# Residual rows of a hybrid decoder layer: turned by VectorE in the up product in place of TensorE after the cross attention, and another order of the last output pair

## The chip, the cores and the metric

The kernel runs on one core of a Trainium2 chip. The metric is device time in microseconds of one execution, as the median of several runs. Before the change it is 1285.01 us (three runs, 1284.41 to 1285.12). One further execution was profiled; the trace that is quoted below comes from it.

## The reference, cut to what matters

One decoder layer over 1024 tokens of width 1024, all in float32: a token mixer (linear attention beside sliding-window attention), a cross attention to 256 memory tokens, a gated MLP with a causal convolution of width 3, and a last RMSNorm. What bears on the change is the end of it:

```python
h = h + concat([o_gla, o_swa]) @ w_out
h = h + cross_attn(rms_norm(h, norm_cross), rms_norm(mem, norm_mem), w_q_c, w_k_c, w_v_c, w_o_c)
h = h + conv_ffn(rms_norm(h, norm_ffn), w_up, conv_w, conv_b, w_down)   # u = h @ w_up; conv; silu(gate) * val; @ w_down
return rms_norm(h, norm_final)
```

The `h` after the second line, called h2 in the kernel, is used twice: normalised, as the input of the up product, and as it is, as the residual that is added to the down product.

## The kernel before, in words

**Layout.** Activations are kept transposed: eight tiles of 128 features x 1024 tokens (`self.h2[0..7]`). The down product comes out with tokens on the partitions, so its residual is wanted in rows: token tile x features. The kernel turns h2 into that form and stores it in a DRAM tensor `h2_d` (eight tiles of 128 tokens x 1024 features), from which the down product's `snapshot` loads 128x512 pieces late in the program.

**Products.** Every matrix product is made of three passes of `fp32r` matmuls on a high and a low part (high x high, high x low, low x high), 128x512 each. Most weights go through a block scheme with seven products of half size in place of eight (Strassen-Winograd): `out_pair` computes two feature tiles of h2 with seven products named "1" to "7", each of 12 matmuls, in the order of a string; `up_winograd` does the same for a gate tile and a value tile of the MLP.

**Cross attention's output.** `cross_out` runs `out_pair` for the pairs j = 1, 2, 3 (tiles 2j and 2j+1; pair 0 was done before). Each pair uses three PSUM banks of a role ("F" or "S", three banks each), and the products that add to an earlier one share its bank. After each product a generator `between` gives other work a step. In the kernel before these steps are calls of `out_rows`: four TensorE transposes 128x128 into the bank of role "T" (L1604), a ScalarE copy to SBUF (L1607) and a POOL DMA to `h2_d` (L1608). There are 16 such calls (8 tiles, 2 halves): twelve lie in the three pairs and four in the eight steps behind them.

Behind the pairs stands the first half (tokens 0 to 511) of the first gate and value tiles of the MLP, not by blocks: eight steps k, each of 2 banks x 3 matmuls (L149 to L151), on h2 that is scaled with the gain but not yet with the row factor. Between the steps stand the remaining transposes, `rstd_half` (the row factors of 512 tokens: 8 small matmuls, L213, then a chain of small VectorE and ScalarE operations, L183 to L191) and `broadcast_rows` (8 small matmuls, L205, and a ScalarE copy to the tile `bc`, L207). Then `ffn_norm` scales the h2 tiles in place with `bc` (VectorE, L1700) and splits them into high and low parts (ScalarE L110 and L113, VectorE L111 and L114); the half with tokens 512 to 1023 is used first, by `up_plain`.

**The up product.** For j = 2 to 21 a block: PE runs the seven products of a gate and a value tile (84 matmuls, L1790). ScalarE and VectorE empty the banks (L1833 to L1845), run the convolution (L1852, L1854), the SiLU and the gate (L1863, L1864), and POOL stores the result to `g_d` (L1865). In the same block they prepare weights: SP loads two tiles of 512 KB (`g`, L1753, and `v`, L1754) into a pool `st` of three buffers, ScalarE and VectorE split them and their sums into high and low parts (L110, L111; sums L1771 to L1776). A load waits until its buffer's last reader is done. PSUM banks alternate between the roles "F" and "S" from block to block.

**What sets the order.** In the stages around `out_pair` the order on TensorE is that in which the code calls; a scheduler of the framework orders the other engines, and all engines in the up product. Each engine then runs its list in that order and waits at semaphores. SP and POOL hold their DMA issues in one list each. The pool `pre` has six buffers of 128x1024; in the kernel before they hold the first operands of the down product.

Of the kernel before, what the change touches and what calls it, by code (L numbers as in the profile page):

```python
# [28 lines left out]
P = 128  # L29
# [32 lines left out]
class Layer:  # L62
# [1484 lines left out]
        product(1, 1, 1)  # L1547
        yield

    def out_pair(self, j, weights, h, tmp, role, order, between):  # L1550


        nc = self.nc
# [1 line left out]
        b11, b21, b22, w1, w2, w3, w4 = weights  # L1555
        left = dict(zip("1234567", (b11, b21, b22, w4, w1, w2, w3)))
        right = dict(zip("1234567", (self.wo[n] for n in ("a11", "a12", "s4", "a22", "s1", "s2", "s3"))))
        banks = [self.bank(role) for _ in range(3)]
        at = dict(zip(order, (0, 1, 0, 2, 0, 2, 0) if j == 1 else (0, 1, 2, 0, 1, 2, 0)))
        t0, t1 = slice(0, 512), slice(512, 1024)  # L1560
        v1, u2, s5 = (tmp("c", [P, 512], bufs=3) for _ in range(3))

# [33 lines left out]
                out(0, t1, ps, v1, ALU.subtract)  # L1596
            next(between, None)

    def out_rows(self, tile, half, tmp):

        nc = self.nc
        ps = self.bank("T")
        for i in range(4):
            nc.tensor.transpose(ps[:, i * P:(i + 1) * P], self.h2[tile][:, (4 * half + i) * P:(4 * half + i + 1) * P],  # L1604
                                self.ident)
        t = tmp("h2r", [P, 4, P], bufs=2)
        nc.scalar.copy(out=t, in_=ps)  # L1607
        nc.gpsimd.dma_start(out=self.h2_d[4 * half:4 * half + 4, :, tile * P:(tile + 1) * P].rearrange("i p c -> p i c"),  # L1608
                            in_=t)

    def cross_out(self, new, tmp, o8, weights, bc):


        nc = self.nc
        self.h2_d = self.dram.tile([NT, P, T], F32, name="h2_d")
        rf = self.small("rstd", [P, NT])
        u = []
        last = NK // 2 - 1

        def rows(j):  # L1620
            for tile in (2 * j, 2 * j + 1):
                for half in range(2):
                    self.out_rows(tile, half, tmp)
                    yield

        def turn(j, which):

            hi, lo = (new("q", [P, 2, 512], F32R, 8) for _ in range(2)) if which[0] == 0 else u.pop()
            for i in which:
                self.split(self.h2[2 * j + i][:, 0:512], hi[:, i], lo[:, i], self.v("norm_ffn", 2 * j + i))  # L1630
            u.append((hi, lo))

        def first_rows():
            g = rows(0)
            for step in (0, 1, 1, 0, 1, 1):
                if step:
                    next(g)
                yield

        def last_rows():  # L1640
            g = rows(last - 1)
            next(g)
            yield
            next(g)
            turn(0, (0, 1))
            yield
            next(g)
            turn(1, (0, 1))
            yield
            next(g)  # L1650
            turn(2, (0, 1))
            yield
            yield
            turn(last, (0,))
            yield
            yield

        for j in range(1, last + 1):
            self.out_tiles(o8)
            self.out_pair(j, weights, self.h2[2 * j:], tmp, "FS"[j % 2], "1426573" if j == 1 else "1652734",  # L1660
                          first_rows() if j == 1 else rows(j - 1) if j < last else last_rows())
            if j < last:
                *_, weights = self.out_weights(j + 1, new)
            if j == last - 1:
                weights = [weights, self.plain_weights(0)]
                weights, plain = weights
        turn(last, (1,))
        banks = [self.bank("F") for _ in range(2)]
        g = rows(last)
        between = {0: lambda: self.rstd_half(rf, self.ss, 0), 1: lambda: next(g), 2: lambda: self.rstd_half(rf, self.ss, 1),  # L1670
                   3: lambda: self.broadcast_rows(rf, bc, (0,), role="S"),
                   4: lambda: self.broadcast_rows(rf, bc, (1,), role="S"), 5: lambda: next(g), 6: lambda: next(g),
                   7: lambda: next(g)}
        for k in range(NK):
            hi, lo = u[k // 2]
            for (wh, wl), ps in zip(plain, banks):
                self.mm3(ps, wh[:, k], wl[:, k], hi[:, k % 2], lo[:, k % 2], k == 0, k == NK - 1)
            between[k]()
        return plain, banks


# [176 lines left out]
    def ffn_up(self, j, us, new):  # L1858

        nc = self.nc  # L1860
        yg = self.conv(us[0], j, new)
        yv = self.conv(us[1], NJ + j, new)
        last = nc.scalar.activation(out=yg, in_=yg, func=AF.Silu)  # L1863
        nc.vector.tensor_tensor(out=yg, in0=yg, in1=yv, op=ALU.mult)  # L1864
        nc.gpsimd.dma_start(out=self.g_d[j], in_=yg)  # L1865
        return last

# [297 lines left out]
    def run(self):  # L2165
# [40 lines left out]
        with self.banks(F=3, S=3, T=1, O=1):  # L2206
# [13 lines left out]
            with self.pool("a", "right") as anew, self.pool("u", "right") as new, ExitStack() as wxs:  # L2220
# [26 lines left out]
                with self.pool("xy") as xnew:  # L2247
                    for j in range(NPLAIN, NJ):
                        if j > NPLAIN:
                            *_, weights = ahead if j == NPLAIN + 1 else self.up_weights(j, wnew)  # L2250
                            us = self.up_winograd(j, weights, new, xnew)
                        if j == NJ - 1:
                            down = self.ffn_down(pre, hcnew)
                            next(down)
# [31 lines left out]
```

## Time and profile before

| what | value |
|---|---|
| median of the runs | 1285.01 us (1284.41 to 1285.12) |
| the profiled execution | 1285.49 us |
| its span in the trace | 1283.8 us |
| PE busy | 1269.5 us, 99% of the span |
| VectorE (DVE) busy | 989.2 us, 77% |
| ScalarE (ACT) busy | 632.8 us, 49% |
| GpSimd (POOL) busy | 114.2 us, 9% |
| DMA | 159.79 MB, 124 GB/s in the mean |
| the three output pairs | 572.6 to 635.6 us from the span's start |
| the eight steps behind them | 635.6 to 651.9 us |
| the up product by blocks | about 685 to 1060 us, 19.04 us each |

The profiled execution is 1.7 us longer than its span; the trace has no row for what lies around the span. PE is the queue of matmuls, PEld the loading of their weights. A row of the timeline has the start, the length, engine and line, tiles (out<-in), and in square brackets how long the engine sat idle before and what it waited for. Matmuls are pipelined: a single one has a length of 0.39 us, though the next starts 0.227 us later, so distances of starts say more than lengths.

### The profile page before, as it was taken

Reading aid. Unit: us, or ns where it says so; the run is one execution under the profiler, and the core shown is the slowest. Engines: PE = TensorE matmul, PEld = TensorE weight load, DVE = VectorE, ACT = ScalarE, POOL = GpSimd, SP = SyncE. Lnnn points to the kernel's source line nnn. Section 1 sums busy time; section 2 is a strip of 40 time slices with the busy share of each in tenths; the row PEclk is TensorE's granted clock in tenths of the full one; section 3 lists DMA queues with packets and bytes.
Section 4 is the critical chain, followed back from the end, with each engine's and each line's share of the span. In section 5 each row is a group of like instructions: output and inputs, shape, how many; then the busy total and the mean of one; then the engine's idle time right before and its main releaser. Section 6 shows DMA issues by size and latency. Waiting matters only on the chain.

```text
span 1283.8 us, 17649 instructions
## 1 busy us (share of the span) xinstructions
PE 1269.5 (99%) x6619; PEld 1059.5 (83%) x6619; DVE 989.2 (77%) x1704; ACT 632.8 (49%) x1127; POOL 114.2 (9%) x194
## 2 busy tenths in 40 slices
PE   8999999999999999999999999999999999999997
PEld 8887777888888888888888888888888888888886
DVE  6848764358657876896898988888888876999687
ACT  5525445336534534864556544344344444454455
POOL 1400111101122000001131000000000000000001
PEclk9999999999999999999999999999999999999999
DMA  7641211238754354243365434222322339610204
GB/s 227 186 122 56 73 58 58 70 132 295 223 156 132 119 167 169 105 141 119 118 146 118 151 102 131 86 72 90 96 68 82 99 113 340 236 66 9 74 19 155
DMA packets 138605, 159.79 MB, mean 124 GB/s; under 512 B 16289, under 2 KB 100438, under 8 KB 138518
## 3 DMA queue, kind: packets, MB, share of 16 engines
q1 hardware_dynamic: 122678, 111.02, 27.6%
q0 software_dynamic: 15680, 47.36, 11.4%
q8 instruction: 52, 0.85, 0.3%
q14 instruction: 35, 0.29, 0.1%
q10 hardware_dynamic: 160, 0.27, 0.1%
HBM read 113.26 MB, written 42.48 MB: 121 GB/s over the span
## 4 chain that ended last, share of the span: by engine, by line
PE 97%; DVE 1%; ACT 1%; DMA 0%; issue 0%; SPq 0%; DVEq 0%; ACTq 0%
PE psS L1790 15%; PE psF L1790 14%; PE psF L149 8%; PE psF L150 7%; PE psF L151 7%; PE psF L1940 6%; PE psS L1940 6%; PE psF L1291 5%; PE psS L1568 3%; PE psS L149 3%; PE psS L151 3%; PE psS L150 3%; PE psO L1940 2%; PE psT L1940 2%; PE psF L1568 1%; PE psO L149 1%
## 5 line engine op out<-in xcount | busy, mean ns | idle before, releaser
L110 ACT CAST w<-st 128x1024 fp32r<-128x1024 f32 (+1 forms) x147 | 125.9, 858 | 212.9 <-PE psF L150 41.1
L111 DVE TENSOR_TENSOR w<-st,w 128x1024 fp32r<-128x1024 f32 (+1 forms) x147 | 144.0, 981 | 55.5 <-ACT w L110 55.4
L1854 DVE SCALAR_TENSOR_TENSOR uy<-uy,vec,uy 128x1023 f32<-128x1023 f32 (+1 forms) x88 | 111.9, 1278 | 0.7 <-ACT uy L1852 0.4
L1790 PE MATMUL psS<-a,w 128*128 128x512 f32 x384 | 92.4, 389 | 0.0
L1940 PE MATMUL psF<-w,w 128*128 128x512 f32 x318 | 88.9, 389 | 0.0
L1940 PE MATMUL psS<-w,w 128*128 128x512 f32 x312 | 87.4, 389 | 0.0
L1790 PEld LDWEIGHTS psS<-a,w 128*128 128x128 f32 x384 | 72.1, 188 | 14.9
L149 PE MATMUL psF<-xh,w 128*128 128x512 f32 x208 | 83.0, 399 | 0.0
L151 PE MATMUL psF<-xh,w 128*128 128x512 f32 x208 | 81.5, 392 | 0.0
L150 PE MATMUL psF<-xl,w 128*128 128x512 f32 x208 | 81.2, 390 | 0.0
L1790 PE MATMUL psF<-a,w 128*128 128x512 f32 x336 | 80.7, 389 | 0.0
L1790 PEld LDWEIGHTS psF<-a,w 128*128 128x128 f32 x336 | 63.1, 188 | 13.1
L1940 PEld LDWEIGHTS psF<-w,w 128*128 128x128 f32 x318 | 59.7, 188 | 12.4
L1940 PEld LDWEIGHTS psS<-w,w 128*128 128x128 f32 x312 | 58.6, 188 | 12.1
L1852 ACT ACTIVATE uy<-uy,vec 128x1024 f32<-128x1024 f32 x44 | 54.8, 1246 | 21.1 <-DVE uy L1845 17.8
L1790 PE MATMUL psS<-act,wx 128*128 128x512 f32 x252 | 60.5, 389 | 0.0
L1790 PE MATMUL psS<-act,w 128*128 128x512 f32 x240 | 58.0, 389 | 0.0
L1790 PE MATMUL psF<-act,w 128*128 128x512 f32 x240 | 57.8, 390 | 0.0
L1790 PEld LDWEIGHTS psS<-act,wx 128*128 128x128 f32 x252 | 47.3, 188 | 9.8
L1790 PE MATMUL psF<-act,wx 128*128 128x512 f32 x228 | 54.8, 389 | 0.0
L1790 PEld LDWEIGHTS psF<-act,w 128*128 128x128 f32 x240 | 45.0, 188 | 9.8 <-ACT o L1815 0.5
L1790 PEld LDWEIGHTS psS<-act,w 128*128 128x128 f32 x240 | 45.1, 188 | 9.3
(574 smaller groups left out, 3071.6 us busy)
## 6 DMA issues: line engine op xcount, KB each, us to landing
st<-in_w_up_dram SPq DMA_DIRECT2D x44, 512.0 KB, 3.7
g_d<-uy POOLq DMA_DIRECT2D x22, 512.0 KB, 2.9
act<-in_w_down_dram SPq DMA_DIRECT2D x12, 512.0 KB, 9.7
st<-g_d SPq DMA_DIRECT2D x10, 512.0 KB, 3.8
res<-g_d SPq DMA_DIRECT2D x10, 512.0 KB, 9.2
st<-in_w_in_dram SPq DMA_DIRECT2D x9, 512.0 KB, 6.8
xt_d<-pts POOLq DMA_DIRECT2D x16, 256.0 KB, 5.4
ow_d<-pts POOLq DMA_DIRECT2D x32, 128.0 KB, 2.8
```

Source lines behind the costliest of these rows:

```text
L110: h = nc.scalar.copy(out=hi, in_=src)
L111: l = nc.vector.tensor_tensor(out=lo, in0=src, in1=hi.bitcast(F32), op=ALU.subtract)
L149: mm(out, lhsT=lh, rhs=rh, start=start, stop=False, skip_group_check=joined)
L150: mm(out, lhsT=lh, rhs=rl, start=False, stop=False, skip_group_check=joined)
L151: mm(out, lhsT=ll, rhs=rh, start=False, stop=stop, skip_group_check=joined)
L1291: mm(ps[n], lhsT=left[n][l][:, q], rhs=self.qa[right[n]][q][r], start=new and q == 0 and i == 0, stop=new and q == 3 and i == 2, skip_grou ...
L1568: mm(ps, lhsT=left[n][l][:, q], rhs=right[n][q][r], start=new and q == 0 and i == 0, stop=new and q == 3 and i == 2, skip_group_check=not new)
L1790: self.nc.tensor.matmul(ps, lhsT=b[l][:, q], rhs=a[q][r], start=first and q == 0 and n == 0, stop=first and q == 3 and n == 2, skip_group_ ...
L1852: nc.scalar.activation(out=y, in_=u, func=AF.Identity, scale=self.v("cw2", j), bias=self.v("conv_b", j))
L1854: nc.vector.scalar_tensor_tensor(out=y[:, s:], in0=u[:, :T - s], scalar=self.v(nm, j), in1=y[:, s:], op0=ALU.mult, op1=ALU.add)
L1940: nc.tensor.matmul(ps[i], lhsT=g[:, l, tk], rhs=w[:, r], start=first and k == 0 and m == 0, stop=first and k == n - 1 and m == 2, skip_gro ...
```

## The change

The TensorE transposes, their ScalarE copies and the stores of `out_rows` are gone. In their place:

- `cross_out` stores the eight h2 tiles as they are (features x tokens, 512 KB each) to a new DRAM tensor `h2t_d`, by POOL, behind the last pair.
- In the up product's blocks j = 6 to 13, behind the gate's multiplication of that block, `row_form` takes one tile k = j - 6: SP loads it from `h2t_d` into a `pre` buffer, VectorE transposes the 32x32 squares inside it into a second `pre` buffer (two instructions 128x512), and POOL issues eight DMAs that put the squares at their places in `h2_d`. Each of those DMAs moves 32 partitions x 16 runs of 32 floats, that is 512 runs of 128 bytes, 64 KB. A buffer of `pre` is now used by `row_form` first and by the down product's loads after it.
- The last output pair (j = 3) runs in the order "1657243" in place of "1652734", with product 4 in a bank of role "T". The outputs for tokens 512 to 1023 are then complete one product earlier.
- In the eight steps behind it the row factors of the second half (tokens 512 to 1023) come behind k = 2 and their broadcast behind k = 4; those of the first half behind k = 5 and k = 7.

```diff
-    def out_pair(self, j, weights, h, tmp, role, order, between):
+    def out_pair(self, j, weights, h, tmp, role, order, homes, between):
...
-        banks = [self.bank(role) for _ in range(3)]
-        at = dict(zip(order, (0, 1, 0, 2, 0, 2, 0) if j == 1 else (0, 1, 2, 0, 1, 2, 0)))
+        banks = [self.bank(r) for r in (role, role, role, "T")[:max(homes) + 1]]
+        at = dict(zip(order, homes))
...
-    def out_rows(self, tile, half, tmp):
-        nc = self.nc
-        ps = self.bank("T")
-        for i in range(4):
-            nc.tensor.transpose(ps[:, i * P:(i + 1) * P], self.h2[tile][:, (4 * half + i) * P:(4 * half + i + 1) * P],
-                                self.ident)
-        t = tmp("h2r", [P, 4, P], bufs=2)
-        nc.scalar.copy(out=t, in_=ps)
-        nc.gpsimd.dma_start(out=self.h2_d[4 * half:4 * half + 4, :, tile * P:(tile + 1) * P].rearrange("i p c -> p i c"),
-                            in_=t)
+    def row_form(self, k, pre):
+        nc = self.nc
+        src, dst = (pre("pre", [P, T], F32, 6) for _ in range(2))
+        nc.sync.dma_start(out=src, in_=self.h2t_d[k])
+        rows = self.h2_d.rearrange("i (b r) c -> r (i b) c", r=32)
+        for h in range(2):
+            sl = slice(512 * h, 512 * h + 512)
+            nc.vector.transpose(out=dst[:, sl], in_=src[:, sl])
+            for a in range(4):
+                c = k * P + 32 * a
+                nc.gpsimd.dma_start(out=rows[:, 16 * h:16 * h + 16, c:c + 32],
+                                    in_=dst[32 * a:32 * a + 32, sl].rearrange("r (b s) -> r b s", s=32))
...
-            self.out_pair(j, weights, self.h2[2 * j:], tmp, "FS"[j % 2], "1426573" if j == 1 else "1652734",
-                          first_rows() if j == 1 else rows(j - 1) if j < last else last_rows())
+            self.out_pair(j, weights, self.h2[2 * j:], tmp, "FS"[j % 2],
+                          *(("1426573", (0, 1, 0, 2, 0, 2, 0)) if j == 1 else ("1652734", (0, 1, 2, 0, 1, 2, 0))
+                            if j < last else ("1657243", (0, 1, 2, 1, 0, 3, 2))), turns() if j == last else iter(()))
...
+        for k in range(NK):
+            nc.gpsimd.dma_start(out=self.h2t_d[k], in_=self.h2[k])
...
-        between = {0: lambda: self.rstd_half(rf, self.ss, 0), 1: lambda: next(g), 2: lambda: self.rstd_half(rf, self.ss, 1),
-                   3: lambda: self.broadcast_rows(rf, bc, (0,), role="S"),
-                   4: lambda: self.broadcast_rows(rf, bc, (1,), role="S"), 5: lambda: next(g), 6: lambda: next(g),
-                   7: lambda: next(g)}
+        between = {2: lambda: self.rstd_half(rf, self.ss, 1), 4: lambda: self.broadcast_rows(rf, bc, (1,), role="S"),
+                   5: lambda: self.rstd_half(rf, self.ss, 0), 7: lambda: self.broadcast_rows(rf, bc, (0,), role="S")}
...
+                        if 6 <= j < 6 + NK:
+                            with self.tc.issue_after(self.gated.ins):
+                                self.row_form(j - 6, pre)
```

The scheduler moves rows with it. Line numbers of the changed program are smaller from here on (L1700 is L1683, L1835 is L1818, L1864 is L1847, L1754's sums L1771 to L1776 are L1754 to L1759). The first place is VectorE where the row factors of the two halves are made, behind the last pair. Before (`rs_v`, `rs_t` and `rstd` are the row factors, `o` the h2 tiles, `bc` the broadcast factors, `act` the low parts):

```order
L189 TENSOR_TENSOR rs_t_6418<-rs_t_6418,rs_v_6417 128x4
L190 TENSOR_SCALAR rs_t_6418<-rs_t_6418 128x4
L191 TENSOR_TENSOR rstd_5874<-rs_y_6419,rs_t_6418 128x4
L188 TENSOR_TENSOR rs_t_6453<-rs_y_6454 128x4
L189 TENSOR_TENSOR rs_t_6453<-rs_t_6453,rs_v_6452 128x4
L190 TENSOR_SCALAR rs_t_6453<-rs_t_6453 128x4
L191 TENSOR_TENSOR rstd_5874<-rs_y_6454,rs_t_6453 128x4
L1700 SCALAR_TENSOR_TENSOR o_5736<-o_5736,vec,bc_5870 128x512
```

After:

```order
L1683 SCALAR_TENSOR_TENSOR o_5738<-o_5738,vec,bc_5870 128x512
L183 TENSOR_SCALAR rs_v_6382<-psO_6377 128x4
L111 TENSOR_TENSOR act_6436<-o_5736,act_6435 128x512
L111 TENSOR_TENSOR act_6436<-o_5738,act_6435 128x512
L188 TENSOR_TENSOR rs_t_6383<-rs_y_6384 128x4
L1683 SCALAR_TENSOR_TENSOR o_5876<-o_5876,vec,bc_5870 128x512
L189 TENSOR_TENSOR rs_t_6383<-rs_t_6383,rs_v_6382 128x4
L1683 SCALAR_TENSOR_TENSOR o_5878<-o_5878,vec,bc_5870 128x512
L190 TENSOR_SCALAR rs_t_6383<-rs_t_6383 128x4
L111 TENSOR_TENSOR act_6438<-o_5876,act_6437 128x512
L191 TENSOR_TENSOR rstd_5875<-rs_y_6384,rs_t_6383 128x4
```

Before, the row factors of both halves stand together, ahead of all scaling. After, those of the first half (`rs_v_6382` to the second `rstd_5875`) stand between scalings and splits of the second half's tiles.

The second place is VectorE in one block of the up product (`c` and `uy` are the emptying of the banks and the convolution, `st` the loaded weights, `w` and `wx` their low parts). Before:

```order
L1835 TENSOR_TENSOR c_7965<-psF_7968,c_7964 128x512
L1864 TENSOR_TENSOR uy_7927<-uy_7927,uy_7931 128x1024
L1771 TENSOR_TENSOR st_8073<-st_8073 128x512
L1775 TENSOR_TENSOR st_8073<-st_8073,st_8072 128x512
L1776 TENSOR_TENSOR st_8072<-st_8072,st_8073 128x512
L111 TENSOR_TENSOR w_8093<-st_8072,w_8092 128x1024
L1839 TENSOR_TENSOR c_7966<-psF_7968,c_7964 128x512
L111 TENSOR_TENSOR wx_8089<-st_8073,wx_8088 128x1024
L1841 TENSOR_TENSOR uy_7963<-psF_7969,c_7966 128x512
```

After:

```order
L1818 TENSOR_TENSOR c_7752<-psS_7755,c_7751 128x512
L1847 TENSOR_TENSOR uy_7714<-uy_7714,uy_7718 128x1024
L1607 STREAM_TRANSPOSE pre_7849<-pre_7848 128x512 x2
L1754 TENSOR_TENSOR st_7873<-st_7873 128x512
L1758 TENSOR_TENSOR st_7873<-st_7873,st_7872 128x512
L1759 TENSOR_TENSOR st_7872<-st_7872,st_7873 128x512
L1822 TENSOR_TENSOR c_7753<-psS_7755,c_7751 128x512
L111 TENSOR_TENSOR wx_7889<-st_7873,wx_7888 128x1024
L111 TENSOR_TENSOR w_7893<-st_7872,w_7892 128x1024
L1824 TENSOR_TENSOR uy_7750<-psS_7756,c_7753 128x512
```

The two transpositions stand right behind the gate's multiplication, and the split of `w`, whose end frees a buffer for the next load, comes two instructions later, behind the emptying L1822 and the split of `wx`.

The third place is SP's queue over three of these blocks. Before:

```order
L1754 DMA st_7269<-in_w_up_dram 128x8x128
L1753 DMA st_7402<-in_w_up_dram 128x8x128
L1886 DMA pre_9542<-g_d 128x2x512
L1754 DMA st_7403<-in_w_up_dram 128x8x128
L1753 DMA st_7536<-in_w_up_dram 128x8x128
```

After:

```order
L1736 DMA st_7578<-in_w_up_dram 128x8x128
L1603 DMA pre_7554<-h2t_d 128x1024
L1737 DMA st_7579<-in_w_up_dram 128x8x128
L1736 DMA st_7725<-in_w_up_dram 128x8x128
L1603 DMA pre_7701<-h2t_d 128x1024
L1737 DMA st_7726<-in_w_up_dram 128x8x128
```

The load of a tile of h2 stands between the loads of the gate's and of the value's weights, and the down product's first loads, which shared these places before, stand behind all eight tiles.

More of the change, by code (lines that the diff above doesn't have):

```diff
@@ L1615, in cross_out @@
         self.h2_d = self.dram.tile([NT, P, T], F32, name="h2_d")
+        self.h2t_d = self.dram.tile([NK, P, T], F32, name="h2t_d")
         rf = self.small("rstd", [P, NT])
@@ L1618, in cross_out @@
         last = NK // 2 - 1
[L1620 to L1624, printed above, removed]
         def turn(j, which):
@@ L1631, in turn, with turns @@
             u.append((hi, lo))
[L1633 to L1637, printed above, removed]
-                yield
[L1640 to L1652, printed above, removed]
+        def turns():
+            yield
+            for j in range(3):
+                turn(j, (0, 1))
+                yield
             yield
@@ L1667, in cross_out @@
         turn(last, (1,))
+        for k in range(NK):
+            nc.gpsimd.dma_start(out=self.h2t_d[k], in_=self.h2[k])
         banks = [self.bank("F") for _ in range(2)]
-        g = rows(last)
-        between = {0: lambda: self.rstd_half(rf, self.ss, 0), 1: lambda: next(g), 2: lambda: self.rstd_half(rf, self.ss, 1),
-                   3: lambda: self.broadcast_rows(rf, bc, (0,), role="S"),
-                   4: lambda: self.broadcast_rows(rf, bc, (1,), role="S"), 5: lambda: next(g), 6: lambda: next(g),
-                   7: lambda: next(g)}
+        between = {2: lambda: self.rstd_half(rf, self.ss, 1), 4: lambda: self.broadcast_rows(rf, bc, (1,), role="S"),
+                   5: lambda: self.rstd_half(rf, self.ss, 0), 7: lambda: self.broadcast_rows(rf, bc, (0,), role="S")}
         for k in range(NK):
@@ L1677, in cross_out @@
                 self.mm3(ps, wh[:, k], wl[:, k], hi[:, k % 2], lo[:, k % 2], k == 0, k == NK - 1)
-            between[k]()
+            if k in between:
+                between[k]()
         return plain, banks
@@ L1863, in ffn_up @@
         last = nc.scalar.activation(out=yg, in_=yg, func=AF.Silu)
-        nc.vector.tensor_tensor(out=yg, in0=yg, in1=yv, op=ALU.mult)
+        self.gated = nc.vector.tensor_tensor(out=yg, in0=yg, in1=yv, op=ALU.mult)
         nc.gpsimd.dma_start(out=self.g_d[j], in_=yg)
```

## The prediction

> **What bounds the kernel now.** I read the page first: busy time by engine, then the chain that ended last.
>
> ```profile
> PE 1269.5 (99%) x6619; PEld 1059.5 (83%) x6619; DVE 989.2 (77%) x1704; ACT 632.8 (49%) x1127; POOL 114.2 (9%) x194
> ...
> PE 97%; DVE 1%; ACT 1%; DMA 0%; issue 0%; SPq 0%; DVEq 0%; ACTq 0%
> ```
>
> PE sets the time: it is busy for 99% of the span and makes 97% of the chain. Work taken off PE is worth its full length; work added elsewhere costs only where it makes PE wait. So I ask two things: what leaves PE, and which of the added or moved steps can come too late for it. The places are then read from the timelines: PE's in the output pairs and the eight steps, VectorE's and SP's in one block of the up product.
>
> **The change part by part. 1: transpositions leave PE.** PE's timeline at the start of the three pairs, at the eight steps and behind them, and last the group of the removed matmuls (lines by form, 570 to 680 us):
>
> ```profile
> 572.62 4.24 PE L1568 MATMUL psS<-act,w 128*128 128x512 f32 x18
> 576.71 1.53 PE L1568 MATMUL psS<-q,w 128*128 128x512 f32 x6
> 578.07 0.60 PE L1604 MATMUL psT<-ident,o 128*128 128x128 f32 x4
> 578.42 3.01 PE L1568 MATMUL psS<-act,w 128*128 128x512 f32 x12
> 581.27 0.60 PE L1604 MATMUL psT<-ident,o 128*128 128x128 f32 x4
> ...
> 635.59 0.39 PE L149 MATMUL psF<-q,w 128*128 128x512 f32 x1
> ...
> 636.95 0.95 PE L213 MATMUL psO<-ones,ss 128*128 128x1 f32 x8
> 637.75 0.48 PE L149 MATMUL psF<-q,w 128*128 128x512 f32 x1
> ...
> 651.90 0.48 PE L149 MATMUL psF<-act,w 128*128 128x512 f32 x1
> ...
> L1604 PE MATMUL psT<-ident,o 128*128 128x128 f32 x64 | 9.6, 272 | 0.0
> ```
>
> The first 18 matmuls take 576.71 - 572.62 = 4.09 us, 0.227 us each. A product of 12 would take 2.72 us; behind a group of four transpositions (578.42 to 581.27) it takes 2.85, and the group itself 0.35. So a group costs 0.35 + 0.13 = 0.48 us, and 16 groups 7.7 us. The three pairs check this: 3 x 84 x 0.2267 = 57.13 us of products, and they take 635.59 - 572.62 = 62.97 us. The twelve groups there are 5.84 us, which I take as saved in full: no product there waits in the trace, and PE then advances by 9% against VectorE, which is busy for 15.9 of the last 21 us of that stretch (a window with the busy time of PE, PEld, DVE, ACT and POOL, the PE clock, the DMA share and GB/s):
>
> ```profile
> 614.60:635.60 21.00, 21.00 (x102) 17.34 (x101) 15.91 (x22) 12.59 (x21) 3.02 (x4) 1.00 0.42 129
> ```
>
> The last pair's other order has the same seven products.
>
> The eight steps take 651.90 - 635.59 = 16.31 us, of which four groups are 1.92. Without them they take 14.4, if nothing waits.
>
> **2: the first half's row factors.** Now something can wait there. The chain from row sums to scaled tiles as it runs now (VectorE, ScalarE, PE):
>
> ```profile
> 642.02 0.16 DVE L183 TENSOR_SCALAR rs_v<-psO 128x4 f32<-128x4 f32 x1 [1.05 <-PE psO L213]
> 643.29 0.16 DVE L191 TENSOR_TENSOR rstd<-rs_y,rs_t 128x4 f32<-128x4 f32 x1
> 643.32 1.05 PE L205 MATMUL psS<-ident,rstd 128*128 128x128 f32 x8
> 644.40 0.58 ACT L207 COPY bc<-psS 128x512 f32<-128x512 f32 x1 [1.75 <-PE psS L205]
> 645.02 4.73 DVE L1700 SCALAR_TENSOR_TENSOR o<-o,vec,bc 128x512 f32<-128x512 f32 x7 [1.57 <-ACT bc L207]
> 649.67 1.89 DVE L111 TENSOR_TENSOR act<-o,act 128x512 fp32r<-128x512 f32 x3
> ```
>
> I count from the start of the steps. Steps are 1.36 us (6 x 0.227); L213 and L205 take 0.80 each, and the step behind each 0.095 more. The second half's broadcast ends at 8.5, so its copy (0.58) lets VectorE scale from 9.4 on. The first half's row sums end at about 10.9, and its broadcast stands behind k = 7, at 13.6. The factor chain alone would be ready by 12.4 (642.02 to 643.45 is 1.43 us). But in the new order its five instructions stand between seven instructions 128x512 of the second half, 0.66 us each for a scaling (4.65 / 7) and 0.6 for a split. Laid out from 9.4: two scalings to 10.75, the first factor instruction to 10.95, two splits to 12.15, one small one, a scaling to 13.0, a small one, a scaling to 13.85, a small one, a split to 14.65, the last small one to 14.9. So PE waits 14.9 - 13.6, about 1.35 us, ahead of the first half's broadcast. The steps then end near 15.85 in place of 16.31: 0.46 saved, not 1.92. The bounds are no wait (the splits let the small ones by) and 2.0. Work behind it hangs on the second half's tiles, which come as early as the steps allow; SP and POOL have nothing queued behind the wait. Sum so far: 5.84 + 0.46 = **6.3 us**.
>
> ScalarE's 16 copies and POOL's 16 stores are off the path, worth nothing. The eight new stores of 512 KB are like those of `g_d`, 2.9 us to landing: the last tiles are complete some 3 us into the steps, so stored by 7, and no tile is scaled in place before 9.4.
>
> ```profile
> g_d<-uy POOLq DMA_DIRECT2D x22, 512.0 KB, 2.9
> ```
>
> **3: two transpositions per block on VectorE.** A window of about two blocks (columns as above), then rows of the block in it, VectorE first, two PE starts last:
>
> ```profile
> 805.00:845.00 40.00, 40.00 (x178) 33.15 (x177) 33.60 (x39) 16.51 (x18) 1.06 (x2) 1.00 0.25 79
> ...
> 824.42 0.68 DVE L1835 TENSOR_TENSOR c<-psS,c 128x512 f32<-128x512 f32 x1
> 825.03 1.21 DVE L1864 TENSOR_TENSOR uy<-uy,uy 128x1024 f32<-128x1024 f32 x1
> ...
> 829.41 1.23 DVE L111 TENSOR_TENSOR w<-st,w 128x1024 fp32r<-128x1024 f32 x1 [1.12 <-ACT w L110]
> ...
> 832.29 0.68 DVE L1841 TENSOR_TENSOR uy<-psS,c 128x512 f32<-128x512 f32 x1
> 834.81 0.69 DVE L1843 TENSOR_TENSOR uy<-psS,c 128x512 f32<-128x512 f32 x1 [1.84 <-PE psS L1790]
> ...
> 826.45 0.39 PE L1790 MATMUL psS<-act,wx 128*128 128x512 f32 x1
> ...
> 834.61 0.62 PE L1790 MATMUL psS<-act,w 128*128 128x512 f32 x2
> ```
>
> PE is full; VectorE has 6.4 us of 40 free. No transposition on VectorE is in this trace. Nearest is a TENSOR_TENSOR 128x512: 0.68 long, the next 0.61 later (824.42 to 825.03). [...] I take 0.6 each, since each element is read and written once in both: 1.2 us a block. Two waits absorb that: 1.12 us ahead of the split at 829.41, and 1.64 us between L1841's end (832.97) and the matmul that reuses its bank (834.61). They are free up to (1.12 + 1.64) / 2 = 1.38 us each; at that price the cover is gone, and each further us costs 8 us. The emptying L1835 stands ahead of them (end 825.10, reuse at 826.45: 1.35 us in hand).
>
> **4: the next weight load.** The value's weights load when the split of `w` is done; here the queue of SP and ScalarE:
>
> ```profile
> 830.67 0.37 SPq L1754 DMA_DIRECT2D st<-in_w_up_dram  x1
> ...
> 837.30 0.62 ACT L110 CAST w<-st 128x512 fp32r<-128x512 f32 x1 [0.46 <-PE psS L1790]
> 838.79 1.25 ACT L1852 ACTIVATE uy<-uy,vec 128x1024 f32<-128x1024 f32 x1 [0.87 <-DVE uy L1845]
> 840.04 1.06 ACT L1863 ACTIVATE uy<-uy 128x1024 f32<-128x1024 f32 x1
> ...
> 840.47 1.28 DVE L1854 SCALAR_TENSOR_TENSOR uy<-uy,vec,uy 128x1023 f32<-128x1023 f32 x1
> ...
> st<-in_w_up_dram SPq DMA_DIRECT2D x34, 512.0 KB, 3.7
> ```
>
> Now the load goes out at 830.67, 6.6 us ahead of its use, and lands in 3.7. After, the split ends at about 832.5 (1.2 for the transpositions, 0.6 for the emptying that overtakes it), so 4.7 us remain. ScalarE has 0.87 idle behind the use and the convolution reads its result 0.43 after it is there: 1.3 more. The load is free up to a landing of 6.0 us; each us above it costs about 1 us in each of 8 blocks, less once the 1.35 in hand.
>
> **5: the short runs.** Just then POOL issues eight stores with 512 runs of 128 bytes. For issue and price per piece:
>
> ```profile
> L1608 POOL DMA_DIRECT2D h_d<-h2r x16 | 12.1, 757 | 179.9 <-ACT h2r L1607 161.9 <-ACT rs_y L185 10.2 <-ACT sq L1513 3.2
> ...
> q0 software_dynamic: 335, 1.11, 14.2%
> ...
> q1 hardware_dynamic: 3130, 0.79, 99.2%
> ...
> q0 software_dynamic: 468, 0.85, 71.4%
> ...
> 682.82 0.62 ACT L110 CAST w<-st 128x512 fp32r<-128x512 f32 x1 [4.18 <-DMA st<-in_w_up_dram]
> ```
>
> A store of 512 pieces holds POOL for 0.76 us, so eight go out from 827 to 833. What a run costs has three rows (queue answers over 577 to 600, 44 to 48 and 676 to 684 us: packets, MB, share of 16 engines). Stores in pieces of 512 bytes: 14.2% x 16 x 23 / 335 = 156 ns for a packet of 3.3 KB, 24 ns a piece. Reads of 252 bytes with the engines full: 99.2% x 16 x 4 / 3130 = 20 ns. Accumulating DMAs, which read what they write: 195 ns for 1.8 KB, 2.3 times as much per byte as the first. So a run costs 20 to 55 ns, 32 runs per engine and DMA 0.65 to 1.8 us, and a block's eight 5.2 to 14 us. At 20 to 24 the queue keeps pace with POOL, and the load at 832.5 meets one or two DMAs, 3.7 + 1.5 = 5.2 us: free. At 55 it finds 14 - 5.6 = 8.4 us queued, lands in up to 12 and costs up to 8 x 6.1 - 1.35 = 47 us. I take 24, the store among the three rows. The load at 676.63 that ran beside the accumulating DMAs landed in 6.1 us (682.82 less its issue), just at the limit.
>
> [...]
>
> **Rivals.** (a) The short runs delay the weights. If a run costs more than some 30 ns, the load at 832.5 lands later than 6.0 us. At 7.5, between the row of 6.1 and the bound of 12, it costs 8 x 1.5 - 1.35 = 10.7 us: 1285.5 - 6.3 + 10.7 = 1289.9 profiled, a median near **1289.4**, slower. For it: the load's room shrinks from 6.6 to 4.7 us. Against it: the DMA share of the window is 0.25, and the 252-byte row.
> (b) No wait at the first half's broadcast, as the splits come later or the small instructions earlier: 5.84 + 1.92 = 7.8 saved, median **1277.3**.
> (c) Some of the blocks lose a few tenths each, by (a) at 6.3 us or by the splits' new order: half of the gain goes, **1280 to 1284**.
> (d) Transpositions at 2 x 0.6 x 1.5 or more, say 2.0 us each: 8 x 1.24 - 1.35 = 8.6 lost, **1287.3**, slower.
>
> **How the numbers follow.** The profiled execution is 1285.49, 0.48 above the median. 1285.49 - 6.3 = 1279.2; less 0.48 the median forecast is **1278.7 us**. Chances: forecast 0.60, (b) 0.12, (c) 0.11, (a) 0.13, (d) 0.04. About 0.2% (2.6 us) is what a measurement of this kernel can tell: below 1282.4 is faster, above 1287.6 slower. Faster: 0.60 + 0.12 + a third of (c), 0.75; slower: most of (a) and half of (d), 0.15; the rest 0.10. The range goes from 1276.8, below (b), to 1285.6, which takes in (c) and leaves most of (a) and (d) out; the forecast's own is 1277.3 to 1280.
>
> **What would show it.** Right: PE's distance from the first pair's start to the steps falls to 57.1 us; the steps take 15.8, with one wait of 1 to 2 us on VectorE ahead of the second L205; blocks 6 to 13 stay at 19.04 us; transpositions of 0.6 to 0.7 us. Wrong by (a): blocks of over 19.04, ScalarE waiting for the DMA of `st` and landings over 6 us; by (d): transpositions over 1.4 us; by (b): no wait ahead of that L205. Wrong at all would be a wait in the pairs.

## The result and the profile after

The changed kernel takes 1321.85 us (median of five, 1318.9 to 1322.61), the kernel before 1284.96 on the same chip. The ratio is 1.0282, interval 1.0267 to 1.0297: slower by 36 us, where 6 us faster was forecast. The profiled execution took 1318.9 us, its span is 1317.2, 33.4 us longer than before.

The same two lines of the page as before, busy time and chain:

```profile
PE 1275.9 (97%) x6555; PEld 1061.1 (81%) x6555; DVE 999.2 (76%) x1720; ACT 624.9 (47%) x1111; POOL 148.7 (11%) x250
...
PE 80%; DVE 7%; issue 6%; DMA 3%; ACT 2%; POOL 1%; SPq 0%; DVEq 0%; ACTq 0%; POOLq 0%
```

PE made 97% of the chain and now makes 80; the rest went to engines that PE waits for. First, where the gain is. PE's timeline of the changed kernel at the start of the pairs, at the steps, behind them and at the first block of the up product:

```profile
571.77 4.24 PE L1568 MATMUL psS<-act,w 128*128 128x512 f32 x18
...
628.89 0.39 PE L149 MATMUL psF<-q,w 128*128 128x512 f32 x1
...
642.50 0.39 PE L149 MATMUL psF<-act,w 128*128 128x512 f32 x1
...
644.09 1.05 PE L205 MATMUL psS<-ident,rstd 128*128 128x128 f32 x8
...
676.07 0.39 PE L1773 MATMUL psS<-a,w 128*128 128x512 f32 x1
```

and the last of these places in the kernel before:

```profile
684.67 0.39 PE L1790 MATMUL psS<-a,w 128*128 128x512 f32 x1
```

The pairs take 57.12 us in place of 62.97 (5.85 saved), and from the steps to the first block it is 47.18 in place of 49.08 (1.90 saved): 7.75 us in all. The pairs also begin 0.85 us earlier, for which no run gives a reason. Then the up product gives back 42, and the three make the 33.4 us. From block start to block start PE takes 19.04 us in every block before; after, seven blocks from 810 us on take 24.21, 23.93, 24.50, 24.29, 25.74, 28.07 and 24.58 us, together 42.0 more than 7 x 19.04. The blocks ahead and behind are 19.04, but for the first two, whose products are interleaved: 38.76 for both in place of 38.42. What waits in the slow blocks, from the waits (engine, line, releaser; us in total, times, longest), and in the last line SP's queue alone, 900 to 970 us:

```profile
PE psS L1773 <- ACT c L1816: 14.2, 4, 3.8
PE psF L1773 <- ACT c L1816: 13.2, 3, 6.6
...
POOL h_d L1610 <- issue: 135.0, 55, 5.8
...
ACT uy L1835 <- DMA g_d<-uy: 28.5, 5, 5.9
...
SPq L1869 <- DMA h_d<-pre: 50.6, 10, 14.4
```

Five of the seven slow blocks come about as the next rows show, the last two in another way. One of the five in the timelines (VectorE, POOL, ScalarE, PE; `h_d` is the profile's name for the residual tensor):

```profile
845.01 1.22 DVE L1847 TENSOR_TENSOR uy<-uy,uy 128x1024 f32<-128x1024 f32 x1
846.14 1.30 DVE L1607 STREAM_TRANSPOSE pre<-pre 128x512 f32<-128x512 f32 x2
...
844.17 0.66 POOL L1610 DMA_DIRECT2D h_d<-pre  x1 [1.90 <-issue]
846.72 0.65 POOL L1610 DMA_DIRECT2D h_d<-pre  x1 [1.89 <-issue]
...
856.89 0.66 POOL L1610 DMA_DIRECT2D h_d<-pre  x1 [3.19 <-issue]
860.61 0.65 POOL L1610 DMA_DIRECT2D h_d<-pre  x1 [3.06 <-issue]
861.25 0.58 POOL L1848 DMA_DIRECT2D g_d<-uy  x1
...
864.61 1.24 ACT L1835 ACTIVATE uy<-uy,vec 128x1024 f32<-128x1024 f32 x1 [5.85 <-DMA g_d<-uy]
866.71 0.56 ACT L1816 COPY c<-psS 128x512 f32<-128x512 f32 x1
...
867.32 3.23 PE L1773 MATMUL psS<-a,w 128*128 128x512 f32 x7 [3.55 <-ACT c L1816]
```

The short-run stores do not follow each other at 0.66 us: the next starts 2.55 us after the last one did, or 3.7 and more. For most of the pauses the profile names nothing that POOL waits for ("issue"). The store at 844.17 lands after 2.2 us, the one at 856.89 after 3.4, and each time the next starts 0.3 us behind the landing, so there is one in flight at a time. Eight of them with their pauses fill POOL for about 24 us of a 19-us block. The store of the gate's product, ready at 846.2, stands behind them and goes out at 861.25. It lands 3 us later, only then is its `uy` buffer free, ScalarE's convolution waits 5.85 us for that, the emptying of a bank (L1816) stands behind the convolution on ScalarE, and PE waits for the bank. The first three blocks with such stores lose nothing, because POOL first has to fall behind.

The last two slow blocks (28.07 and 24.58, together 14.6 of the 42.0) show a second way to PE (POOL, SP, ScalarE):

```profile
932.98 0.65 POOL L1610 DMA_DIRECT2D h_d<-pre  x1 [1.90 <-issue]
...
935.35 0.37 SPq L1869 DMA_DIRECT2D pre<-in_w_down_dram  x1
935.83 0.56 SPq L1737 DMA_DIRECT2D st<-in_w_up_dram  x1
...
941.70 0.62 ACT L110 CAST w<-st 128x512 fp32r<-128x512 f32 x1 [9.49 <-DMA st<-in_w_up_dram]
```

A load of the down product (L1869) needs a `pre` buffer out of which POOL still stores. It goes out at 935.35, when the store of 932.98 has landed, and the next weights (L1737) stand behind it on SP. ScalarE waits 9.49 us for them, and the emptying of a bank is late again. In both ways POOL's lag is what PE ends up waiting for.

### The profile page after: what moved, and what is told of

The parts are those of the page before. It is cut to its first block, busy times and chain, and to the rows that moved or that the text cites. A ratio compares the mean times of both kernels' runs of the same rounds, so it can differ in the third digit from the quotient of the medians.

```text
span 1317.2 us, 17596 instructions
## 1 busy us (share of the span) xinstructions
PE 1275.9 (97%) x6555; PEld 1061.1 (81%) x6555; DVE 999.2 (76%) x1720; ACT 624.9 (47%) x1111; POOL 148.7 (11%) x250
## 4 chain that ended last, share of the span: by engine, by line
PE 80%; DVE 7%; issue 6%; DMA 3%; ACT 2%; POOL 1%; SPq 0%; DVEq 0%; ACTq 0%; POOLq 0%
PE psS L1773 9%; PE psF L1773 7%; PE psF L149 7%; PE psF L150 7%; PE psF L151 7%; PE psF L1923 6%; PE psS L1923 5%; PE psF L1291 5%; PE psS L1568 3%; PE psO L1923 2%; PE psT L1923 2%; PE psS L149 2%; PE psS L151 2%; PE psS L150 2%; DVE uy L1837 2%
## 5 line engine op out<-in xcount | busy, mean ns | idle before, releaser
L1773 PE MATMUL psS<-a,w 128*128 128x512 f32 x384 | 100.0, 412 | 14.2 <-ACT c L1816 14.2
L1773 PEld LDWEIGHTS psS<-a,w 128*128 128x128 f32 x384 | 76.7, 201 | 32.4 <-ACT c L1816 15.9
L1773 PE MATMUL psF<-a,w 128*128 128x512 f32 x336 | 86.1, 408 | 13.2 <-ACT c L1816 13.2
L1773 PEld LDWEIGHTS psF<-a,w 128*128 128x128 f32 x336 | 66.6, 199 | 28.7 <-ACT c L1816 14.5
L1835 ACT ACTIVATE uy<-uy,vec 128x1024 f32<-128x1024 f32 x44 | 54.8, 1245 | 43.5 <-DMA g_d<-uy 28.5
L1610 POOL DMA_DIRECT2D h_d<-pre x64 | 42.0, 656 | 151.0 <-issue 135.0
```

Source lines behind the costliest of these rows:

```text
L1610: nc.gpsimd.dma_start(out=rows[:, 16 * h:16 * h + 16, c:c + 32], in_=dst[32 * a:32 * a + 32, sl].rearrange("r (b s) -> r b s", s=32))
L1773: self.nc.tensor.matmul(ps, lhsT=b[l][:, q], rhs=a[q][r], start=first and q == 0 and n == 0, stop=first and q == 3 and n == 2, skip_group_ ...
L1835: nc.scalar.activation(out=y, in_=u, func=AF.Identity, scale=self.v("cw2", j), bias=self.v("conv_b", j))
```

## Experiments

Three theories: **R**, POOL's queue holds runs up to a limit, and a second store of 512 runs does not fit beside the first; **L**, runs of 128 bytes cost DMA time, as the prediction's rival (a) had it; **D**, each store waits for the one before since all write one tensor. Times are beside the kernel before on the same chip (1285.1 to 1285.8 us).

**Whole runs.** Here the squares do not get to their places in the residual; the number and the size of the stores stay.

```diff
...
-                nc.gpsimd.dma_start(out=rows[:, 16 * h:16 * h + 16, c:c + 32],
-                                    in_=dst[32 * a:32 * a + 32, sl].rearrange("r (b s) -> r b s", s=32))
+                nc.gpsimd.dma_start(out=self.h2_d[k, 32 * a:32 * a + 32, sl], in_=dst[32 * a:32 * a + 32, sl])
```

> The changed kernel, but each of the eight stores of a block writes its 32 partitions in runs of 2048 bytes (to other places of the residual tensor, so the residual that is added at the end is wrong). Number of stores, bytes, POOL's order and the waits of the program are as in the change; only the number of runs per store falls from 512 to 32. Theory R (POOL's queue holds runs up to a limit between one and two of these stores, so the next store waits until the last has landed): no such limit is met, stores go out at 0.6 us each, the loss of 42 us in blocks 7 to 13 is gone, 1284.96 - 8 = about 1277. Theory L (short runs cost DMA time): also about 1277. Theory D (each store waits for its predecessor, whatever its runs are, since all write one tensor): still over 2 us per store, 8 of them over 19 us a block, time stays near 1320.

Measured: 1277.89 us (1276.84 to 1278.66), ratio 0.9937 (0.992 to 0.9953). Eight stores of the same bytes cost nothing, to the same tensor (they leave POOL in 3.92 us), so D falls. The number of runs, or their length, is what matters; R and L remain.

**Half stores.**

```diff
+                for q in range(2):
+                    b = 16 * h + 8 * q
-                nc.gpsimd.dma_start(out=rows[:, 16 * h:16 * h + 16, c:c + 32], ...
+                    nc.gpsimd.dma_start(out=rows[:, b:b + 8, c:c + 32], ...
```

> The changed kernel with each store cut in two of 256 runs: 16 stores a block, the same runs of 128 bytes and the same bytes. Theory R: two or three stores fit in the queue at once, 16 of them take 10 to 14 us of a block in place of 20 to 24, the store of the gate's product is no longer late: 1277 to 1285. Theory L: the runs are the same and so is the time, 1320 to 1325. Theory D: 16 x 2.5 = 40 us a block, some 20 us more in each of 8 blocks: about 1440.

Measured: 1277.48 us (1277.23 to 1278.69), ratio 0.9936 (0.9922 to 0.9951); on a further chip with five rounds:

> The same kernel as the run with half stores, on this chip, with more rounds: 1277 to 1278.5, ratio to the kernel before 0.993 to 0.995.

1278.09 us (1277.39 to 1278.7), ratio 0.9944 (0.9932 to 0.9957). All runs of 128 bytes are still there, twice as many stores issue, and the 42 us are gone: L falls as the cause. POOL's timeline shows the limit at work:

```profile
852.53 1.74 POOL L1612 DMA_DIRECT2D h_d<-pre  x3 [0.47 <-issue]
854.74 0.58 POOL L1612 DMA_DIRECT2D h_d<-pre  x1 [0.47 <-issue]
856.78 0.57 POOL L1850 DMA_DIRECT2D g_d<-uy  x1 [1.46 <-DVE uy L1849]
857.51 1.75 POOL L1612 DMA_DIRECT2D h_d<-pre  x3 [0.16 <-issue]
```

Three stores of 256 runs go out back to back, never four. With one of 512 going out and not two, the limit lies between 768 and 1023 runs in flight. In six of the eight blocks the sixteen are done before the gate's product is, and POOL waits 0.75 to 2.6 us for VectorE ahead of the product's store; in the last two it does not wait, so little room is left.

**A larger queue.** The kernel is built with 1024 for `dynamic_dma_scratch_size`; this run has 1280.

```diff
-    nc = bacc.Bacc("TRN2", target_bir_lowering=False, num_devices=1, dynamic_dma_scratch_size=1024)
+    nc = bacc.Bacc("TRN2", target_bir_lowering=False, num_devices=1, dynamic_dma_scratch_size=1280)
...
-        self.tiny = e(tc.tile_pool(name="tiny", bufs=3))
+        self.tiny = e(tc.tile_pool(name="tiny", bufs=2))
...
```

> The changed kernel with its 512-run stores as they are; only the scratch memory that the program reserves per partition for the descriptors of POOL's DMAs is 1280 bytes in place of 1024 (room for it from a pool of small tiles with two buffers in place of three). If theory R holds and this memory is the limit (the run with half stores let three of 256 runs out at once and not four, so the limit lies from 768 to 1023 runs), a quarter more holds 960 to 1279 runs; if that reaches 1024, two 512-run stores are out at once, a block's eight take about 11 us and the time is 1277 to 1279. If the limit is elsewhere, the stores go out one by one as before and the time is 1319 to 1323.

Measured: 1288.12 us, ratio 1.0022 (1.0013 to 1.0032). The stores of 512 runs now go out in twos:

```profile
766.72 1.37 POOL L1610 DMA_DIRECT2D h_d<-pre  x2 [0.22 <-issue]
769.95 1.29 POOL L1610 DMA_DIRECT2D h_d<-pre  x2 [1.86 <-issue]
```

and no block is longer than another. So the reserved memory looks like the limit, as R says. The time did not fall to 1277, though: every block, with or without stores, takes 19.38 us, and the pairs 58.14 in place of 57.12. Whether the smaller pool or the larger queue did that, the next run tells (half stores, queue as before):

```diff
-        self.tiny = e(tc.tile_pool(name="tiny", bufs=3))
+        self.tiny = e(tc.tile_pool(name="tiny", bufs=2))
...
```

> The run with half stores with two buffers in place of three in the pool of small tiles, as the run with the larger queue had it, and the queue's memory at 1024 bytes. That run's matmuls follow each other at 0.2307 us in place of 0.2267 in the pairs and in the up product, which made up its 10 us. If the small tiles are the cause (addresses of all that lies behind them): about 1287. If the larger reserved memory is: 1277 to 1278.5.

Measured: 1287.57 us, ratio 1.0018 (1.0009 to 1.0028), the same as with the larger queue. At its start of the pairs:

```profile
574.45 4.35 PE L1568 MATMUL psS<-act,w 128*128 128x512 f32 x18
578.64 1.54 PE L1568 MATMUL psS<-q,w 128*128 128x512 f32 x6
```

18 matmuls take 4.19 us in place of 4.09: a distance of 0.2328 here, 19.38 / 84 = 0.2307 in the blocks. The pool of small tiles costs the 10 us. It does not move the limit: with the old queue and the small pool, stores of 256 runs still go out three in a row and never four. So what let two stores of 512 runs out is the reserved memory. With the same small pool, 512-run stores in the larger queue (1288.12) and half stores in the old one (1287.57) are within 0.6 us of each other.

**The other way out for the product's store.**

```diff
-        nc.gpsimd.dma_start(out=self.g_d[j], in_=yg)
+        nc.sync.dma_start(out=self.g_d[j], in_=yg)
```

> The changed kernel with the eight 512-run stores per block on POOL as they are; only the store of the gate's product to g_d is issued by SP. If the loss comes by the way that the trace shows (the product's store queues behind the eight, its buffer comes free late, ScalarE's convolution waits for it), blocks return to 19.04 us: POOL's 20 to 24 us a block then runs behind by 1 to 5 us a block, with nothing behind it but its own buffers: 1277 to 1283. If the loss comes by the load of the value's weights or by DMA time, it stays: 1315 or more.

Measured: 1324.43 us, ratio 1.0308 (1.0292 to 1.0323). My expectation of 1277 to 1283 missed. The blocks up to 907 us are all 19.04, as expected, but then two take 35.82 and 47.29, together 45.0 more than 19.04 each. SP's queue, POOL's last store and ScalarE:

```profile
962.97 0.37 SPq L1869 DMA_DIRECT2D pre<-in_w_down_dram  x1
...
963.95 0.38 SPq L1737 DMA_DIRECT2D st<-in_w_up_dram  x1
...
960.54 0.65 POOL L1610 DMA_DIRECT2D h_d<-pre  x1 [1.89 <-issue]
...
923.41 0.62 ACT L110 CAST w<-st 128x512 fp32r<-128x512 f32 x1 [16.95 <-DMA st<-in_w_up_dram]
```

POOL still needs some 200 us for its 64 stores where eight blocks have 152. The down product's first loads (`pre`, L1869) need the buffers out of which POOL stores, stand on SP ahead of the next weights, and hold SP until 962.97, when POOL's last store has landed. So the first waits of the changed kernel are on the gate's product, but the cause is POOL's total; with these waits gone, the loss moves to the way that already costs the changed kernel its last two slow blocks. I had counted POOL's lag as harmless.

**Four stores a block.** A call of `row_form` now takes half a tile: one transposition and its four stores.

```diff
...
-                        if 6 <= j < 6 + NK:
+                        if 4 <= j < 4 + 2 * NK:
                             with self.tc.issue_after(self.gated.ins):
-                                self.row_form(j - 6, pre)
+                                self.row_form((j - 4) // 2, j % 2, pre)
```

> The changed kernel with its 512-run stores on POOL, but four per block over 16 blocks (4 to 19) in place of eight over 8 blocks (6 to 13). One at a time, 64 stores still take about 200 us of POOL's queue in sum. If the loss came because POOL's 24 us a block is more than the block of 19.04, then 12 us a block fits, the store of the gate's product is on time, no block is longer: 1277 to 1279. If each store costs PE by itself (DMA time, contention), the loss stays: about 1320.

Measured: 1279.32 us (1278.4 to 1279.62), ratio 0.9953 (0.9939 to 0.9966).

```profile
801.73 0.57 POOL L1850 DMA_DIRECT2D g_d<-uy  x1 [4.04 <-DVE uy L1849]
802.45 0.67 POOL L1612 DMA_DIRECT2D h_d<-pre  x1
805.69 0.65 POOL L1612 DMA_DIRECT2D h_d<-pre  x1 [2.57 <-issue]
...
812.77 0.65 POOL L1612 DMA_DIRECT2D h_d<-pre  x1 [3.88 <-issue]
820.77 0.57 POOL L1850 DMA_DIRECT2D g_d<-uy  x1 [7.36 <-DVE uy L1849]
```

The stores are as slow as in the changed kernel, one at a time, but four of them and their pauses end by 813.4 and the queue is free before the next product: all these blocks are 19.04. What decides is POOL's time per block against the block's 19.04: 11 to 14 us for the four stores here, about 24 for the eight in the changed kernel.

**Stores on SP.**

```diff
-                nc.gpsimd.dma_start(out=rows[:, 16 * h:16 * h + 16, c:c + 32],
+                nc.sync.dma_start(out=rows[:, 16 * h:16 * h + 16, c:c + 32],
```

> The changed kernel with the eight 512-run stores per block issued by SP in place of POOL. If the limit belongs to POOL's queue alone (its reserved memory), SP sends eight without waiting for a landing: some 3 us of issue and 4 to 6 us of transfer a block, the weight load behind them goes out about as late as before: 1277 to 1282. If runs of 128 bytes themselves keep the queue (theory L), the weight load behind them is late by over 10 us: above 1320.

Measured: 1278.68 us (1278.23 to 1279.22), ratio 0.9949 (0.9936 to 0.9963). Eight stores of 512 runs leave SP in 4.87 us:

```profile
799.76 4.87 SPq L1610 DMA_DIRECT2D h_d<-pre  x8
```

The limit is that of POOL's queue; SP's shows none at this count.

**Short reads in place of short stores**, and with it the old order:

```diff
+        nc.gpsimd.dma_start(out=self.h2_d[k], in_=dst)
...
-            nc.sync.dma_start(out=dst, in_=self.h2_d[t, :, 512 * c:512 * c + 512])
+        src = self.h2_d[4 * c:4 * c + 4].rearrange("k (a r) (b s) -> b r (k a) s", r=32, s=32)
+        for i in range(4):
+            self.nc.sync.dma_start(out=dst[32 * i:32 * i + 32].rearrange("r (q s) -> r q s", s=32), in_=src[4 * t + i])
```

> The changed kernel with another layout of the residual tensor: the transposed tile is stored as it lies in SBUF, one store of 512 KB in runs of 4 KB, and the 16 loads of the down product pick the runs of 128 bytes, four loads of 512 runs in place of one, on SP's queue. R, L and D all expect blocks of 19.04 us throughout and about 1277, if the down product's loads are early enough: PE never waits in the down product before. If short runs are dear on SP's queue too (L), loads of 256 KB take 5 us and more, and PE or VectorE wait in the down product: 1280 to 1290.

Measured: 1281.65 us (1280.4 to 1283.1), ratio 0.9969 (0.9956 to 0.9982): faster than before, but not 1277. The up product is undisturbed; the down product takes 209.88 us in place of 205.36. Four reads of 128x512 in sixteen pieces hold SP, here first and then in the kernel before:

```profile
1084.02 15.32 SPq L1602 DMA_DIRECT2D c<-h_d  x16
```

```profile
1090.87 4.27 SPq L1983 DMA_DIRECT2D c<-h_d  x4
```

and what stands behind them on SP is late (ScalarE, then PE, with short reads):

```profile
1104.65 0.62 ACT L110 CAST w<-st 128x512 fp32r<-128x512 f32 x1 [5.97 <-DMA st<-g_d]
...
1108.49 0.73 PE L1924 MATMUL psF<-w,w 128*128 128x512 f32 x2 [2.15 <-DVE w L111]
```

The order alone, once on this kernel and once on the half stores:

```diff
-                          *(("1426573", (0, 1, 0, 2, 0, 2, 0)) if j == 1 else ("1652734", (0, 1, 2, 0, 1, 2, 0))
-                            if j < last else ("1657243", (0, 1, 2, 1, 0, 3, 2))), turns() if j == last else iter(()))
+                          *(("1426573", (0, 1, 0, 2, 0, 2, 0)) if j == 1 else ("1652734", (0, 1, 2, 0, 1, 2, 0))),
+                          turns() if j == last else iter(()))
...
-        between = {2: lambda: self.rstd_half(rf, self.ss, 1), 4: lambda: self.broadcast_rows(rf, bc, (1,), role="S"),
-                   5: lambda: self.rstd_half(rf, self.ss, 0), 7: lambda: self.broadcast_rows(rf, bc, (0,), role="S")}
+        between = {0: lambda: self.rstd_half(rf, self.ss, 0), 2: lambda: self.rstd_half(rf, self.ss, 1),
+                   3: lambda: self.broadcast_rows(rf, bc, (0,), role="S"),
+                   4: lambda: self.broadcast_rows(rf, bc, (1,), role="S")}
```

> As the run with short reads, but the last output pair in its old order (1652734, three banks) and the row factors of the first half at k = 0, of the second at k = 2, broadcasts at k = 3 and k = 4, as before the change. If the new order is worth something, VectorE's scaling and splitting is late for the plain up product that PE now reaches 1.9 us earlier: 0.5 to 2 us more than the run with short reads. If the order is worth nothing, the same within 0.5 us.

> The run with half stores, but the last output pair and the row factors in the order that they had before the change. From the traces of the two runs with short reads (47.60 against 47.18 us from the steps to the first block): 0.4 us more than with half stores, 1277.9; within 0.5 us of it in any case. If the new order is needed to make use of the steps, 1.4 us more or above.

Measured: 1282.45 us (1279.91 to 1284.85) against 1281.65, and 1277.8 (1277.04 to 1278.6) against 1277.48. In times the order is worth nothing that can be told. In the traces, from the steps to the first block, it is 47.60 and 47.70 us with the old order against 47.18 and 47.17 with the new: about half a microsecond.

**Six transpositions.** The half stores, each transposition three times:

```diff
-            nc.vector.transpose(out=dst[:, sl], in_=src[:, sl])
+            for _ in range(3):
+                nc.vector.transpose(out=dst[:, sl], in_=src[:, sl])
```

> The run with half stores with every transposition done three times (six of 128x512 per block in place of two, 0.61 us each). The prediction gave 2.76 us of cover per block. Six take 3.66: 0.9 us over it in each of 8 blocks, less the 1.35 in hand once, is 5.9 us: 1283. If VectorE has more room than the two waits show, since other work can stand aside, 1277.5. If the transpositions are not covered at all, 2.44 us more per block: 1297.

Measured: 1278.86 us (1278.23 to 1279.46), 0.8 to 1.4 above the two runs of half stores and not 6. Two blocks of the kernel before, then of this one (busy PE, PEld, DVE, ACT, POOL):

```profile
799.25:837.33 38.08, 38.08 (x169) 31.54 (x168) 31.68 (x37) 16.51 (x19) 1.06 (x2) 1.00 0.26 84
```

```profile
792.13:830.56 38.43, 38.37 (x170) 31.48 (x168) 37.26 (x48) 16.12 (x19) 19.52 (x34) 1.00 0.46 128
```

VectorE had (38.08 - 31.68) / 2 = 3.2 us free in a block, more than the 2.76 that I had counted from two waits, and is at 97% here. Only three blocks are longer, by 0.1 to 0.35 us.

## Why the prediction was wrong, by its own steps

**The step that failed** is in part 5: "A store of 512 pieces holds POOL for 0.76 us, so eight go out from 827 to 833." They took about 24 us in place of these 6. The 757 ns are the row of L1608, and are right for a store that meets an empty queue. Two of L1608 in the kernel before, and the ScalarE copy that makes the operand of the second:

```profile
652.99 0.76 POOL L1608 DMA_DIRECT2D h_d<-h2r  x1 [2.28 <-ACT act L110]
656.01 0.75 POOL L1608 DMA_DIRECT2D h_d<-h2r  x1 [2.26 <-ACT a L113]
...
652.79 0.59 ACT L1607 COPY h2r<-psT 128x512 f32<-128x512 f32 x1
```

They are 3.0 us apart, no two of L1608 lie closer, and none of the sixteen lands in less than 2.7. So none of its rows shows two stores of 512 pieces in flight, and the duration of one issue says nothing about eight in a row. The second store shows the limit itself: its operand is ready at 653.38, the store ahead of it lands at 655.7, and it goes out at 656.01. The releaser that the row names, L113, does not write the operand. The numbers that I needed were in view. I should have carried one landing per store, 8 x 2.7 = 22 us against a block of 19.04, as the other end of the range for POOL's time. The prediction also followed the eight stores only to the DMA engines: that the product's store stands behind them on POOL, and the down product's loads behind their buffers, has no term in it.

**Rival (a)** had the right sign and the right part of the change, and the wrong mechanism. It let the runs delay the value's weights from a price of 30 ns a run on. That the upper end of its loss, 47 us, lies near the 42 is luck. What a run does cost in the changed kernel, from POOL's queue (packets, MB, share of 16 engines), 770 to 965 us, and for the subtraction 790 to 870 us of the stores on SP, where POOL's queue holds the stores to `g_d` alone:

```profile
q0 software_dynamic: 3136, 8.26, 18.0%
```

```profile
q0 software_dynamic: 576, 2.10, 7.0%
```

The second gives 7.0% x 16 x 80 / 4 = 22 us of engine time for a store to `g_d`. The first, 18.0% x 16 x 195 = 562, less eight of those, leaves 382 us for 61 stores: 6.3 us each over 16 engines, 12 ns a run, half of the 24 that I took. Whole runs, 790 to 870 us of that run with 32 stores and four to `g_d`:

```profile
q0 software_dynamic: 1600, 4.20, 17.5%
```

17.5% x 16 x 80 = 224, less 4 x 22.4, leaves 4.2 us a store. So the same 64 KB take more engine time in runs of 128 bytes than in runs of 2048, 6.3 against 4.2 us, and this did not decide. What decided is how many runs POOL's queue lets out: in the run with the larger queue, 1280 in place of 1024 lets two stores of 512 runs out in 1.37 us in place of one.

**Term 1**, the transpositions in the pairs: forecast 5.84 us, measured 5.85. **Term 2**, the steps: forecast 0.46, measured 1.90. Rival (b) had this saving, but not its reason: the small instructions on VectorE did not come earlier by much (the last ends at 643.43, 14.5 us from the start of the steps, where I laid out 14.9). I let PE wait for them at the second broadcast. PE's order has seven matmuls of the plain up product (642.50 to 644.09) ahead of that broadcast, so PE has work until the factors are ready. I had read the order of one engine, not of both. **Term 3**, two transpositions at 0.6 us: 1.30 us for both, 0.61 each, covered; the cover was larger than I said. **Part 4**, the weight load: the first five slow blocks do not come from it. In the last two ScalarE does wait for `st`, 9.49 and 6.67 us, which is a sign that I had given to rival (a); but the load of 935.83 lands after 5.8 us, inside my 6.0, and what is late is its issue, behind the down product's load.

The sum without the failed step, 7.75 us, is what the half stores show: 1285.75 less 1277.48 is 8.3, and 1285.17 less 1278.09 is 7.1. The best version found is therefore the change with stores of 256 runs, 0.9944 of the time before.

## What to carry to other kernels

A DMA's issue time on POOL, read where stores lie far apart, was no rate here (0.76 us of issue at 3.0 us apart, then 2.55 us and more from start to start): ask how many are in flight at once in the trace, and carry one landing per store as the price until a row shows two overlapping. POOL's in-order queue got more work per block than a block lasts, about 24 us against 19.04: the users of that queue and of its buffers became late in turn, and moving one of them away only moved the wait (1324.43 us against 1321.85). Reading a stall needs the order on both engines, the one that is late and the one that waits, since the second may have other work ahead.

## What was not expected of the hardware

PE's seven waits in the slow blocks cost more than their length. One wait of the changed kernel in PE's timeline, the stretch behind it and the one after that (windows: busy PE, PEld, DVE, ACT, POOL, granted clock, DMA share, GB/s):

```profile
842.85 4.60 PE L1773 MATMUL psF<-a,w 128*128 128x512 f32 x12 [3.01 <-ACT c L1816]
...
842.85:847.25 4.40, 4.40 (x12) 3.50 (x13) 4.40 (x6) 0.00 (x0) 1.18 (x2) 0.61 0.21 30
847.30:863.00 15.70, 15.70 (x71) 13.01 (x70) 11.33 (x14) 5.48 (x6) 3.26 (x6) 1.00 0.47 138
```

Here the granted clock is 0.61 in the mean behind the wait, and 12 matmuls take 4.4 us in place of 2.72. Behind the seven waits it is 0.50 to 0.65, for 4.2 to 5.3 us. By the starts in PE's timeline the seven waits hold PE up for 28.6 us, and the slow matmuls behind them for 13.5 more: together the 42 us. One slow product stands behind each of the seven waits, behind the fifth a second of 3.05 us; the shortest wait is the one of 3.01 us above, the longest 6.63 us, and the window behind the slow product above is at 1.00 again.

The number of buffers in the pool of small tiles changes the distance of matmuls: with two in place of three it is 0.2307 us in place of 0.2267 in the up product, and unchanged in the down product (205.42 against 205.36 us). The order of work is the same as in the second run of half stores, and the granted clock is 0.998 in both; no run shows the reason.
